# A hybrid convolution and gated-attention block: attention's output product as two sets of seven block products, with ScalarE in program order from the mixer's sets on

## The chip, the cores and the metric

The kernel runs on one core of one Trainium2 chip. The metric is the device time of one execution in microseconds (us), as the median of several runs. TensorE multiplies, VectorE (DVE) and ScalarE (ACT) work on tiles of 128 partitions, GpSimd (POOL) and SyncE (SP) mostly issue DMAs.

## The reference

One block works on 512 positions of width 1024, all in float32: a half-weighted SwiGLU, a mixer, a second SwiGLU and a last norm.

```python
x = x + 0.5 * swiglu(rmsnorm(x, g1), w_gu1, w_down1)        # 1024 -> 2 x 2816 -> 1024
h = rmsnorm(x, gm)
cb, cc, cu, q, k, v, g_lr, r, ga, gb = split(h @ w_in)
y_conv = (cb * causal_short_conv(cc * cu, conv_w)) @ w_out_conv
o = gla_chunked(q, k, v, log_sigmoid(g_lr @ gate_w_up + gate_b) / 16)   # 4 heads, chunks of 64
o = o * rsqrt(mean(o * o) + eps) * gla_norm_g                # per head, 256 wide
y_gla = (o * silu(r)) @ w_out_gla                            # 1024 x 1024
x = x + (sigmoid(ga) * y_conv + sigmoid(gb) * y_gla) @ w_o
x = x + 0.5 * swiglu(rmsnorm(x, g2), w_gu2, w_down2)
out = rmsnorm(x, gf)
```

## The kernel before, in words

**Layout.** Everything is held transposed: a tile has 128 features on its partitions and 512 positions along it. Each float32 operand is split into a rounded high part and the rest (`h`, `l`), and a product is three matmuls: high by high, high by low, low by high. ScalarE makes the high part (a CAST), VectorE the low part (a subtraction). For weights these are the tiles `wh` and `wl` (lines 328 and 329), three buffers each; for activations the tiles `op`, 14 buffers.

**Two kinds of product.** A *single* (`mm_single`, lines 351 to 359) makes 128 output features for all 512 positions: 8 blocks of the inner dimension by 3 matmuls, 24 matmuls of 512 columns, with one unit of split weights of 128 x 1024. A *set* (`Set` and `Operands`) makes 512 output features as a 2 by 2 block product by Winograd's form: seven block products named m1, p2, q6, p5, q7, p4, p3 instead of eight, each 24 matmuls of 256 columns (line 520) with a unit of split weights of its own. Some weights are sums of blocks: one sum is made by VectorE (line 313), three by DMAs that add in place, issued by POOL (line 303). Sums of activation blocks are made in place by VectorE (`Operands.sum`). Three of the products are copied out of PSUM by ScalarE (line 525); VectorE adds the quarters of the output (`quarter`, lines 1219 to 1230).

**The plan.** `PLAN` and `STEPS` list the weight units in the order of use. `Weights.take` issues the load, the split and the sums of a unit up to two steps ahead. SP issues all loads of weights. The order of one engine's instructions is otherwise made by a scheduler that works from modelled times; only in the last stage of the kernel is it written by hand (`tc.manual_schedule`).

**The mixer.** q, k and v come as singles and wide products. Then twelve sets follow (`MSETS`): the gates ga and gb, the convolution's inputs, cb and r. Attention's four heads are worked between the steps of these sets by hooks: `gates(h)`, `decays`, `scale(h)`, `scores(h)`, `state(h)`, `output(h)`, `squares(h)`. `gates` is a chain on ScalarE of Abs, Exp and Ln with a table load, and a scan on VectorE. The gates ga and gb are written to DRAM by DMAs that ScalarE issues. The last two sets are r: silu of r multiplies `O`, attention's output.

After the sets, w_out_conv is eight singles whose operands are the split of `Y` (line 1282: tiles `op` from tiles `y`). Each result is multiplied by sigmoid(ga), which SP loads into a temporary of the pool `tp` (six buffers). Meanwhile `O` is normalised by `r64`. Then w_out_gla is eight singles whose operands are the split of `O`; each result is multiplied by sigmoid(gb) and added into `m`. During the second of them x is reloaded from DRAM (`xs`) by POOL's DMAs. The split of `m` feeds w_o: one group of four outputs, then four singles. w_o's results are added to x.

Of the kernel before, what the change touches and what calls it, by code (L numbers as in the profile page):

```python
# [20 lines left out]
KF = DFF // P  # L21
HEADS = 4
# [168 lines left out]
def block_kernel(ctx: ExitStack, tc: tile.TileContext, xT, vecs, gf, gup, wgl, wts, out):  # L191
    nc = tc.nc
# [3 lines left out]
    front = ctx.enter_context(tc.tile_pool(name="front", bufs=1))  # L196
# [49 lines left out]
    x = [XS[0][:, k] for k in range(KD)]  # L246
# [237 lines left out]
    def newton_rsqrt(r, v, s, q):  # L484
        nc.scalar.activation(s, v, AF.Sqrt)
        nc.vector.reciprocal(s, s)
        nc.vector.tensor_tensor(out=q, in0=s, in1=s, op=ALU.mult)
        nc.vector.tensor_tensor(out=q, in0=q, in1=v, op=ALU.mult)
        nc.vector.tensor_scalar(out=q, in0=q, scalar1=-0.5, scalar2=1.5,
                                op0=ALU.mult, op1=ALU.add)  # L490
        nc.vector.tensor_tensor(out=r, in0=s, in1=q, op=ALU.mult)

    def mul(out_, a, b, eng=None):
        (eng or nc.vector).tensor_tensor(out=out_, in0=a, in1=b, op=ALU.mult)
# [359 lines left out]
    def mixer(norm, nxt):  # L854
        xh, xl = norm.h, norm.l
        cpool = pools["small"]
        xs = dram.tile([KD, P, S], F32, tag="xs", name="xs")
        gates_d = {n: dram.tile([KD, P, S], F32, tag=n, name=n) for n in ("ga", "gb")}
# [4 lines left out]
        Y = [tile_of("y", [P, 2, S + 2]) for _ in range(4)]  # L863
# [4 lines left out]
        def two(i):  # L868
            return flat(i).rearrange("p (e t) -> p e t", e=2)
# [6 lines left out]
        def G_tile(i, dtype=F32):  # L876
# [13 lines left out]
            out=maskf, in_=maskf, pattern=[[1, P]], compare_op=ALU.is_ge, fill=0.0,  # L890
# [21 lines left out]
        for i in range(6):  # L912
# [3 lines left out]
                                in1=gup_w[R2 : 2 * R2].bitcast(F32), op=ALU.subtract)  # L916
# [19 lines left out]
        def evac_k(h, o):  # L936
# [7 lines left out]
                                in1=glr[2 * R2 : R3].bitcast(F32), op=ALU.subtract)  # L944
# [27 lines left out]
        E, M, KS, EX, QS = (G_tile(i) for i in range(5))  # L972
# [6 lines left out]
        vs = cpool.tile([P, 16 * HEADS], F32, tag="vs", name="vs")  # L979
# [86 lines left out]
        O = [two(0), two(1), None, None]  # L1066
# [62 lines left out]
        OB = []  # L1129
# [45 lines left out]
        late = []  # L1175

        def finish_late():
            while late:
                late.pop(0)()
# [38 lines left out]
        def quarter(s, p):  # L1218

            bank, v = s.bank, s.v  # L1220
            if p not in ("p2", "q7", "p3"):
                return None
            t = T()
            if p == "q7":
                nc.vector.scalar_tensor_tensor(out=t, in0=bank["c"], scalar=-1.0, in1=v["q7"],
                                               op0=ALU.mult, op1=ALU.subtract)
            else:
                nc.vector.tensor_tensor(out=t, in0=bank["a" if p == "p2" else "c"],
                                        in1=v["m1" if p == "p2" else "q6"], op=ALU.add)
            return t  # L1230
# [42 lines left out]

            return Set(xo, done)

        run_sets(make, hooks=hooks)
        finish_late()


        def split_pair(v):  # L1280
            h, l = (tile_of("op", [P, 2, S], F32R) for _ in range(2))
            nc.scalar.copy(h, v)
            nc.vector.tensor_tensor(out=l, in0=v, in1=h.bitcast(F32), op=ALU.subtract)
            return [(h[:, i], l[:, i]) for i in range(2)]

        def parts(v):
            r = [hl for i in v for hl in split_pair(i)]
            return [a for a, _ in r], [b for _, b in r]

        def gate(name, d):  # L1290
            t = T()
            nc.sync.dma_start(t, gates_d[name][d])
            nc.scalar.activation(t, t, AF.Sigmoid)
            return t

        c_h, c_l = parts([Y[i][:, :, 2:] for i in range(4)])
        m = [two(d // 2)[:, d % 2] for d in range(KD)]

        n64 = [front.tile([P, HEADS * 16], F32, tag=t, name=f"{t}o") for t in
               ("st_v", "st_s", "st_r")]  # L1300
        r64, s64, q64 = n64
        newton_rsqrt(r64, vs, s64, q64)
        og = []
        for d in range(KD):
            t = gate("ga", d)
            yp = mm_single("w_out_conv", KD, d * P, c_h, c_l)
            mul(m[d], yp, t)
            if d % 2 == 0:
                h = d // 2
                tr, orow = E, M  # L1310
                nc.vector.tensor_copy(
                    tr.rearrange("p (b c) -> p b c", c=32),
                    r64[:, 16 * h : 16 * (h + 1)].unsqueeze(2).to_broadcast([P, 16, 32]))
                nc.vector.transpose(orow, tr)
                mul(O[h], O[h], orow.unsqueeze(1).to_broadcast([P, 2, S]))
        og_h, og_l = parts(O)
        m_h, m_l = [], []
        for d in range(KD):
            t = gate("gb", d)
            yp = mm_single("w_out_gla", KD, d * P, og_h, og_l)  # L1320
            if d == 1:
                XS.append(big("X2"))
                x[:] = [XS[-1][:, k] for k in range(KD)]
                for k in range(KD):
                    nc.gpsimd.dma_start(x[k], xs[k])
            mul(t, yp, t)
            nc.vector.tensor_tensor(out=m[d], in0=m[d], in1=t, op=ALU.add)
            if d % 2 == 1:
                for a, b in split_pair(two(d // 2)):
                    m_h.append(a)  # L1330
                    m_l.append(b)

        def evac(d, o):
            nc.vector.tensor_tensor(out=x[d], in0=o, in1=x[d], op=ALU.add)
# [72 lines left out]
```

## Time and profile before

| | |
|---|---|
| median of 3 runs | 1201.32 us (1201.03 to 1201.35) |
| profiled execution, whole | 1202.43 us |
| its span, first to last instruction | 1200.7 us |
| TensorE busy | 1191.5 us, 99% |
| VectorE busy | 799.2 us, 67% |
| ScalarE busy | 578.0 us, 48% |
| DMA | 184.48 MB, 154 GB/s on average |
| matmuls of 256 columns in sets (line 520) | 5040 |
| granted TensorE clock | 0.999 |

The profiled execution has a time of its own, 1202.43 us, of which the span is 1200.7. Views that are quoted later give a start in us from the beginning of the span, then a duration, the engine, the line, the operation, the output and input tiles, and in square brackets how long the engine sat idle before it and what ended that. A matmul's own duration overlaps with the next one's, so the pace of matmuls is read from the times between starts. Stages on the span: the mixer's sets end at 719.95 us, w_out_conv runs from there to 763.5, w_out_gla from 763.5 to 807.0, w_o and FFN2 follow.

### The profile page before, as it was taken

To read this page: it belongs to the slowest core of one execution; us is meant where nothing else is said; L and a number is where in the kernel's file an instruction comes from. 1 tells how busy PE (TensorE), PEld (TensorE's weight loads), DVE (VectorE), ACT (ScalarE), POOL (GpSimd) and SP (SyncE) were. 2 spreads that over 40 slices of the span, in tenths; PEclk is the share of its full clock that TensorE was granted. 3 is DMA by queue.
4 is the path that set the end of the run, shared out by engine and by line. 5 is a ranking of instruction groups with operands and counts; after the bars stand their busy time and mean duration, and the time that the engine had idled before them with its cause. 6 is when DMAs were issued, how large, how long until landed. Compare 5 with 4: busy or idle time off the path is not lost.

```text
span 1200.7 us, 18772 instructions
## 1 busy us (share of the span) xinstructions
PE 1191.5 (99%) x7714; PEld 1090.1 (91%) x7714; DVE 799.2 (67%) x960; ACT 578.0 (48%) x721; POOL 94.9 (8%) x131
## 2 busy tenths in 40 slices
PE   9999999999999999999999999999999999999997
PEld 7899999988888889999999998888889999998886
DVE  7976666832267864858678786455597666675685
ACT  6454454622153455646455464323346444562353
POOL 0011111000010000101101100100001111100100
PEclk9999999999999999999999999999999999999999
DMA  9377777532073316777777766614438777763431
GB/s 342 79 211 182 188 179 191 176 96 71 8 266 112 88 48 163 181 191 190 178 190 176 190 173 209 217 37 140 124 75 205 174 185 173 189 177 108 95 95 70
DMA packets 56741, 184.48 MB, mean 154 GB/s; under 512 B 6384, under 2 KB 10608, under 8 KB 56656
## 3 DMA queue, kind: packets, MB, share of 16 engines
q1 hardware_dynamic: 36912, 124.27, 30.3%
q0 software_dynamic: 15104, 54.53, 24.6%
q10 hardware_dynamic: 4640, 4.49, 1.2%
q8 instruction: 60, 0.98, 0.3%
q14 instruction: 25, 0.20, 0.0%
HBM read 124.55 MB, written 8.39 MB: 111 GB/s over the span
## 4 chain that ended last, share of the span: by engine, by line
PE 98%; ACT 1%; DMA 0%; DVE 0%; SPq 0%; issue 0%; ACTq 0%
PE mm L520 50%; PE mm L358 7%; PE mm L356 7%; PE mm L357 7%; PE mm L380 7%; PE mm L785 3%; PE mm L735 2%; PE mm L736 2%; PE mm L734 2%; PE mm L398 1%; PE mm L399 1%; PE mm L397 1%; PE aux L356 1%; PE aux L358 1%; PE aux L357 1%; PE aux L1076 1%
## 5 line engine op out<-in xcount | busy, mean ns | idle before, releaser
L520 PE MATMUL mm<-op,wh 128*128 128x256 f32 x3360 | 607.8, 284 | 0.3 <-ACT tp L525 0.3
L328 ACT CAST wh<-f 128x1024 fp32r<-128x1024 f32 (+1 forms) x313 | 327.1, 1046 | 490.2 <-PE mm L520 214.3
L329 DVE TENSOR_TENSOR wl<-f,wh 128x1024 fp32r<-128x1024 f32 (+1 forms) x313 | 380.4, 1218 | 251.7 <-ACT wh L328 238.1
L520 PEld LDWEIGHTS mm<-op,wh 128*128 128x128 f32 x3360 | 523.9, 192 | 1.3 <-ACT tp L525 0.5
L520 PE MATMUL mm<-op,wl 128*128 128x256 f32 x1680 | 475.6, 283 | 0.2 <-DVE wl L329 0.2
L520 PEld LDWEIGHTS mm<-op,wl 128*128 128x128 f32 x1680 | 321.8, 192 | 0.5 <-DVE wl L329 0.4
L356 PE MATMUL mm<-op,wh 128*128 128x512 f32 x388 | 151.3, 390 | 0.0
L358 PE MATMUL mm<-op,wl 128*128 128x512 f32 x388 | 151.2, 390 | 0.0
L357 PE MATMUL mm<-op,wh 128*128 128x512 f32 x388 | 151.0, 389 | 0.0
L303 POOL DMA_DIRECT2D f<-f x96 | 82.9, 864 | 845.4 <-DVE wl L329 460.1
L358 PEld LDWEIGHTS mm<-op,wl 128*128 128x128 f32 x388 | 72.8, 188 | 15.2
L357 PEld LDWEIGHTS mm<-op,wh 128*128 128x128 f32 x388 | 72.9, 188 | 15.2
L356 PEld LDWEIGHTS mm<-op,wh 128*128 128x128 f32 x388 | 72.8, 188 | 14.8
L380 PE MATMUL mm<-op,wh 128*128 128x512 f32 x256 | 63.8, 391 | 0.6 <-DVE op L431 0.4
L380 PEld LDWEIGHTS mm<-op,wh 128*128 128x128 f32 x256 | 47.7, 188 | 11.8 <-ACT wh L328 1.1
L525 ACT COPY tp<-mm 128x512 f32<-128x512 f32 x90 | 52.1, 579 | 0.0
L313 DVE TENSOR_TENSOR f<-f,f 128x1024 f32<-128x1024 f32 x32 | 39.1, 1223 | 0.8
L569 DVE TENSOR_TENSOR op<-hid,op 128x1024 fp32r<-128x1024 f32 x21 | 25.7, 1223 | 15.3 <-ACT op L568 15.3
L568 ACT CAST op<-hid 128x1024 fp32r<-128x1024 f32 x21 | 22.0, 1050 | 28.6 <-PE aux L735 20.7
L785 PE MATMUL mm<-wh,op 128*128 128x512 f32 x112 | 34.6, 389 | 0.0
L380 PE MATMUL mm<-op,wl 128*128 128x512 f32 x128 | 34.4, 391 | 0.0
L380 PEld LDWEIGHTS mm<-op,wl 128*128 128x128 f32 x128 | 23.9, 188 | 5.5 <-DVE wl L329 0.4
(252 smaller groups left out, 1152.2 us busy)
## 6 DMA issues: line engine op xcount, KB each, us to landing
f<-wts SPq DMA_DIRECT2D x219, 512.0 KB, 4.2
f<-f POOLq DMA_DIRECT2D x96, 512.0 KB, 5.0
X<-xT SPq DMA_DIRECT2D x8, 256.0 KB, 5.6
xs<-X POOLq DMA_DIRECT2D x8, 256.0 KB, 5.3
ga<-tp ACTq DMA_DIRECT2D x8, 256.0 KB, 4.3
gb<-tp ACTq DMA_DIRECT2D x8, 256.0 KB, 4.1
tp<-ga SPq DMA_DIRECT2D x8, 256.0 KB, 5.9
tp<-gb SPq DMA_DIRECT2D x8, 256.0 KB, 2.6
```

The source lines that it names most:

```text
L303: nc.gpsimd.dma_start(out_, a, accum_op=ALU.add)
L313: nc.vector.tensor_tensor(out=s3, in0=a11, in1=a21, op=ALU.add)
L328: nc.scalar.copy(h[:, :w], raw[:, :w])
L329: nc.vector.tensor_tensor(out=l[:, :w], in0=raw[:, :w], in1=h[:, :w].bitcast(F32), op=ALU.subtract)
L356: nc.tensor.matmul(o, wh, ah, start=first, stop=False)
L357: nc.tensor.matmul(o, wh, al, start=False, stop=False)
L358: nc.tensor.matmul(o, wl, ah, start=False, stop=last)
L380: nc.tensor.matmul(o[c], w[:, s : s + P], a[k], start=k == 0 and j == 0, stop=k == kt - 1 and j == 2)
L520: nc.tensor.matmul(to, ww[:, s], aa[:, t], start=fresh and k == 0 and e == 0 and j == 0, stop=k == 3 and j == 2, skip_group_check=True)
L525: nc.scalar.copy(v, o)
L569: nc.vector.tensor_tensor(out=lv, in0=v, in1=hv.bitcast(F32), op=ALU.subtract)
L785: nc.tensor.matmul(to, aa[:, c], ww, start=fresh and k == 0 and n == 0, stop=k == 3 and n == 2, skip_group_check=True)
```

## The change

w_out_gla becomes two sets of 512 outputs each. Their operands are blocks of `O`, which moves from four tiles to the flat view `Of`, and the sums are made in place in it; the operands m1, p2, p5 are made during w_out_conv. `O` is normalised head by head in the first four singles of w_out_conv, with two pairs of temporaries in turn. gb no longer goes through `tp`: quarters of it are loaded by SP into four fixed tiles (E, M, KS, EX), at steps that the table READ gives, and pass the sigmoid at steps that TAKE gives. The results are multiplied and added by quarters (`gla_add`), and `m` is split when a pair of its blocks is done. x is reloaded by SP after the first set's p3, not by POOL.

And from the mixer's twelve sets to the end of the new ones ScalarE runs in the order in which the code is written: the whole stretch stands under `tc.manual_schedule(engines={ENG.Activation})`. The other engines remain with the scheduler.

```diff
-    for d in range(KD):
-        units(single("w_out_gla", KD, d * P))
+    sets("w_out_gla", [(4 * i * P, (4 * i + 2) * P) for i in range(2)])
...
-        run_sets(make, hooks=hooks)
-        finish_late()
+        with tc.manual_schedule(engines={ENG.Activation}):
+            run_sets(make, hooks=hooks)
+            finish_late()
...
+            Of = OB[0].rearrange("p h e t -> p (h e) t")
+            oo = Operands(lambda j, l: Of[:, 4 * j : 4 * j + 4, half(l)])
+            AT = {3: "m1", 4: "p2", 6: "p5"}
             for d in range(KD):
                 t = gate("ga", d)
                 yp = mm_single("w_out_conv", KD, d * P, c_h, c_l)
                 mul(m[d], yp, t)
-            if d % 2 == 0:
-                h = d // 2
-                tr, orow = E, M
+                if d < HEADS:
+                    tr, orow = (E, M) if d % 2 else (KS, QS)
...
+                if d in AT:
+                    oo.make(AT[d])
+            oo.sum("q6")
-        og_h, og_l = parts(O)
-        for d in range(KD):
-            t = gate("gb", d)
-            yp = mm_single("w_out_gla", KD, d * P, og_h, og_l)
-            if d == 1:
...
-                    nc.gpsimd.dma_start(x[k], xs[k])
-            mul(t, yp, t)
-            nc.vector.tensor_tensor(out=m[d], in0=m[d], in1=t, op=ALU.add)
-            if d % 2 == 1:
-                for a, b in split_pair(two(d // 2)):
...
+            places = {(0, 0): E, (1, 1): M, (1, 0): KS, (0, 1): EX}
...
+            def gla_done(i):
+                def done(s, p):
+                    if not (i == 1 and p in ("q6", "p5", "q7")):
+                        finish_late()
+                    gla_add(i, s, p)
+                    if (i, p) in READ:
+                        fetch_gate(*READ[i, p])
+                    if (i, p) in TAKE:
+                        g = places[TAKE[i, p]]
+                        nc.scalar.activation(g, g, AF.Sigmoid)
+                return done
...
+            def reload():
...
+                    nc.sync.dma_start(x[k], xs[k])
+
+            run_sets(lambda i: Set(oo, gla_done(i)), hooks={(0, "p3"): [reload]})
+            finish_late()
```

Three places of the order that the prediction speaks of follow. Line numbers in the changed kernel are one lower there (327 for 328, 524 for 525, 1283 for 1282).

The first place is ScalarE's order at the end of the mixer's sets. `op<-y` are the high parts of w_out_conv's operands, `op<-O` of attention's output, `tp<-tp` and `tp<-mm` the silus of r, and wh_7073 (wh_7075 in the changed kernel) the first weights of w_out_conv. Before:

```order
L1282 CAST op_7147<-y_3387 128x1024
L1282 CAST op_7151<-y_3388 128x1024
L525 COPY tp_7027<-mm_6844 128x512
L328 CAST wh_7033<-f_6584 128x1024
L1243 ACTIVATE tp_7029<-tp_7029 128x512
L328 CAST wh_7073<-f_7065 128x1024
L1282 CAST op_7456<-O 128x1024
L328 CAST wh_7106<-f_7067 128x1024
L1243 ACTIVATE tp_7062<-tp_7062 128x512
L1237 ACTIVATE tp_7102<-mm_6844 128x512
L328 CAST wh_7170<-f_7069 128x1024
L1243 ACTIVATE tp_7135<-tp_7135 128x512
```

The same stretch of ScalarE in the changed kernel:

```order
L524 COPY tp_7029<-mm_6846 128x512
L1242 ACTIVATE tp_7031<-tp_7031 128x512
L327 CAST wh_7035<-f_6586 128x1024
L1242 ACTIVATE tp_7064<-tp_7064 128x512
L327 CAST wh_7075<-f_7067 128x1024
L1236 ACTIVATE tp_7104<-mm_6846 128x512
L327 CAST wh_7108<-f_7069 128x1024
L1242 ACTIVATE tp_7137<-tp_7137 128x512
L1283 CAST op_7141<-y_3385 128x1024
L1283 CAST op_7145<-y_3386 128x1024
L1283 CAST op_7149<-y_3387 128x1024
L1283 CAST op_7153<-y_3388 128x1024
```

All four casts of `op<-y` moved from ahead of the last copy of the sets (two of them stand still further up in the order before) to behind the last silu, tp_7137.

The second place is the hook `gates(2)` on ScalarE, after the second set's q6. tp_4541 (tp_4543) is q6's copy, wh_4552 (wh_4554) the first weights of the next set, the rows from `aux` to the third `g` the gate's Abs, Exp and Ln. Before:

```order
L328 CAST wh_4552<-f_4307 128x1024
L525 COPY tp_4541<-mm_4368 128x512
L987 ACTIVATE g_492_3614<-aux_4543,vec 128x512
L990 ACTIVATE g_492_3614<-g_492_3614 128x512
L991 ACT_TABLE_LOAD
L991 ACTIVATE g_492_3614<-g_492_3614 128x512
L328 CAST wh_4590<-f_4033 128x1024
L1004 ACT_TABLE_LOAD
```

ScalarE there in the changed kernel:

```order
L524 COPY tp_4543<-mm_4370 128x512
L986 ACTIVATE g_492_3614<-aux_4545,vec 128x512
L989 ACTIVATE g_492_3614<-g_492_3614 128x512
L990 ACT_TABLE_LOAD
L990 ACTIVATE g_492_3614<-g_492_3614 128x512
L327 CAST wh_4554<-f_4309 128x1024
L1249 DMA ga<-tp_4506 128x2x256
L327 CAST wh_4592<-f_4033 128x1024
```

And VectorE beside it in the changed kernel, where the third row is the scan and wl_4555 the low part of those weights:

```order
L987 TENSOR_SCALAR g_493_3615<-aux_4545,vec 128x512
L991 TENSOR_TENSOR g_493_3615<-g_493_3615,g_492_3614 128x512
L992 SCALAR_TENSOR_TENSOR g_492_3614<-reset,g_493_3615 128x512
L328 TENSOR_TENSOR wl_4555<-f_4309,wh_4554 128x1024
L997 TENSOR_TENSOR g_493_3615<-g_492_3614 128x512
```

The next set's first cast went from ahead of the copy to behind the gate's chain, and its low part now stands behind the scan.

The third place is TensorE's order where w_out_conv begins, in the changed kernel. The first row is the last matmul of the sets; mm_7169 is the first output of w_out_conv and mm_7215 the second, op_7141 and op_7142 are the high and low parts of the first operand.

```order
L519 MATMUL mm_6970<-op_4300,wl_7036 128x256
L355 MATMUL mm_7169<-op_7141,wh_7075 128x512
L355 MATMUL mm_7215<-op_7141,wh_7108 128x512
L356 MATMUL mm_7169<-op_7142,wh_7075 128x512
L357 MATMUL mm_7169<-op_7141,wl_7076 128x512
```

One matmul of the second output moved in ahead of the first that needs op_7142; otherwise w_out_conv's order is as before.

More of the change, by code (lines that the diff above doesn't have):

```diff
@@ L1274, in make @@
             return Set(xo, done)
-        run_sets(make, hooks=hooks)
-        finish_late()
[L1280 to L1303, printed above, removed]
@@ L1304, in mixer @@
-        for d in range(KD):
-            t = gate("ga", d)
-            yp = mm_single("w_out_conv", KD, d * P, c_h, c_l)
-            mul(m[d], yp, t)
-            if d % 2 == 0:
-                h = d // 2
-                tr, orow = E, M
[L1311 to L1315, printed above, removed]
@@ L1316, in mixer, with split_pair, parts, gate @@
-        og_h, og_l = parts(O)
-        m_h, m_l = [], []
-        for d in range(KD):
-            t = gate("gb", d)
-            yp = mm_single("w_out_gla", KD, d * P, og_h, og_l)
-            if d == 1:
+        with tc.manual_schedule(engines={ENG.Activation}):
+            run_sets(make, hooks=hooks)
+            finish_late()
+            def split_pair(v):
+                h, l = (tile_of("op", [P, 2, S], F32R) for _ in range(2))
+                nc.scalar.copy(h, v)
+                nc.vector.tensor_tensor(out=l, in0=v, in1=h.bitcast(F32), op=ALU.subtract)
+                return [(h[:, i], l[:, i]) for i in range(2)]
+            def parts(v):
+                r = [hl for i in v for hl in split_pair(i)]
+                return [a for a, _ in r], [b for _, b in r]
+            def gate(name, d):
+                t = T()
+                nc.sync.dma_start(t, gates_d[name][d])
+                nc.scalar.activation(t, t, AF.Sigmoid)
+                return t
+            c_h, c_l = parts([Y[i][:, :, 2:] for i in range(4)])
+            m = [two(d // 2)[:, d % 2] for d in range(KD)]
+            n64 = [front.tile([P, HEADS * 16], F32, tag=t, name=f"{t}o") for t in
+                   ("st_v", "st_s", "st_r")]
+            r64, s64, q64 = n64
+            newton_rsqrt(r64, vs, s64, q64)
+            Of = OB[0].rearrange("p h e t -> p (h e) t")
+            oo = Operands(lambda j, l: Of[:, 4 * j : 4 * j + 4, half(l)])
+            AT = {3: "m1", 4: "p2", 6: "p5"}
+            for d in range(KD):
+                t = gate("ga", d)
+                yp = mm_single("w_out_conv", KD, d * P, c_h, c_l)
+                mul(m[d], yp, t)
+                if d < HEADS:
+                    tr, orow = (E, M) if d % 2 else (KS, QS)
+                    nc.vector.tensor_copy(
+                        tr.rearrange("p (b c) -> p b c", c=32),
+                        r64[:, 16 * d : 16 * (d + 1)].unsqueeze(2).to_broadcast([P, 16, 32]))
+                    nc.vector.transpose(orow, tr)
+                    mul(O[d], O[d], orow.unsqueeze(1).to_broadcast([P, 2, S]))
+                if d in AT:
+                    oo.make(AT[d])
+            oo.sum("q6")
+            m_h, m_l = [None] * KD, [None] * KD
+            places = {(0, 0): E, (1, 1): M, (1, 0): KS, (0, 1): EX}
+            def fetch_gate(i, a, l):
+                d = 4 * i + 2 * a
+                nc.sync.dma_start(pair(places[a, l]), gates_d["gb"][d : d + 2, :, half(l)].rearrange(
+                    "e p t -> p e t"))
+            READ = {(0, "q6"): (1, 0, 0), (1, "m1"): (1, 1, 1), (0, "p3"): (1, 1, 0),
+                    (1, "q6"): (1, 0, 1)}
+            TAKE = {(0, "m1"): (0, 0), (0, "p5"): (1, 1), (0, "q7"): (1, 0), (0, "p4"): (0, 1),
+                    (1, "p5"): (1, 1), (1, "q7"): (0, 0), (1, "p2"): (1, 0), (1, "p4"): (0, 1)}
+            for a, l in places:
+                fetch_gate(0, a, l)
+            def gla_done(i):
[9 more added lines that the diff above has]
+                return done
+            def gla_add(i, s, p):
+                if p not in ("p2", "q7", "p4", "p3"):
+                    return
+                a, l = int(p in ("p4", "q7")), int(p in ("q7", "p3"))
+                d = 4 * i + 2 * a
+                g = places[a, l]
+                if p == "p4":
+                    nc.vector.scalar_tensor_tensor(out=g, in0=s.bank["b"], scalar=-1.0, in1=g,
+                                                   op0=ALU.mult, op1=ALU.mult)
+                else:
+                    mul(g, quarter(s, p), g)
+                y = two(d // 2)
+                nc.vector.tensor_tensor(out=y[:, :, half(l)], in0=y[:, :, half(l)], in1=pair(g),
+                                        op=ALU.add)
+                if p in ("p4", "p3"):
+                    def f():
+                        for j, (b, c) in enumerate(split_pair(y)):
+                            m_h[d + j], m_l[d + j] = b, c
+                    late.append(f)
+            def reload():
@@ L1324, in mixer @@
                 for k in range(KD):
-                    nc.gpsimd.dma_start(x[k], xs[k])
-            mul(t, yp, t)
-            nc.vector.tensor_tensor(out=m[d], in0=m[d], in1=t, op=ALU.add)
-            if d % 2 == 1:
-                for a, b in split_pair(two(d // 2)):
-                    m_h.append(a)
-                    m_l.append(b)
+                    nc.sync.dma_start(x[k], xs[k])
+            run_sets(lambda i: Set(oo, gla_done(i)), hooks={(0, "p3"): [reload]})
+            finish_late()
         def evac(d, o):
```

## The prediction

> **What bounds the kernel now.** I read the page first, its busy times and the chain that ended last.
>
> ```profile
> PE 1191.5 (99%) x7714; PEld 1090.1 (91%) x7714; DVE 799.2 (67%) x960; ACT 578.0 (48%) x721; POOL 94.9 (8%) x131
> PE 98%; ACT 1%; DMA 0%; DVE 0%; SPq 0%; issue 0%; ACTq 0%
> ```
>
> TensorE is busy 99% of the span and 98% of the chain. A busy matmul row says little about how fast matmuls follow each other, so the next view is who TensorE waited for in the whole span.
>
> ```profile
> PE aux L235 <- POOL ones L232: 1.1, 1, 1.1
> PE mm L380 <- DVE op L431: 0.4, 1, 0.4
> PE mm L520 <- ACT tp L525: 0.3, 1, 0.3
> PE mm L520 <- DVE wl L329: 0.2, 1, 0.2
> PE mm L380 <- ACT wh L328: 0.2, 1, 0.2
> ```
>
> That is 2.2 us in all. So the time changes in two ways only: the matmuls' own pace changes, or a wait appears that is not there now. Nothing can be won by removing waits. The pace comes from the chain in order of time and from VectorE's timeline, which shows when each product of the old stage was finished.
>
> ```profile
> 699.91 20.04 PE mm L520 x167
> 719.95 0.23 PE mm L356
> 941.49 20.16 PE mm L520 x168
> ```
>
> ```profile
> 741.77 0.69 DVE L494 TENSOR_TENSOR y<-mm,tp 128x512 f32<-128x512 f32 x1 [3.13 <-PE mm L358]
> 763.53 0.69 DVE L494 TENSOR_TENSOR y<-mm,tp 128x512 f32<-128x512 f32 x1 [2.00 <-PE mm L358]
> 807.05 0.69 DVE L494 TENSOR_TENSOR tp<-mm,tp 128x512 f32<-128x512 f32 x1 [2.89 <-PE mm L358]
> L494 DVE TENSOR_TENSOR tp<-mm,tp 128x512 f32<-128x512 f32 x8 | 5.5, 692 | 17.4 <-PE mm L358 17.4
> ```
>
> The last line groups the old stage's eight evacuations (763.5 to 807.1): every one waited for its matmuls. The mixer's sets end at 719.95 and the next matmul (L356) follows with no gap: call that moment T.
>
> **The matmuls.** Between 763.53 (the last product of w_out_conv) and 807.05 (the eighth of w_out_gla) lie eight products: 43.52 us, or 5.44 each, or 0.227 per matmul of 512 columns. A whole set in FFN2 is 168 matmuls of 256 columns in 20.16 us, 0.120 each. Two sets are 336 matmuls, 40.32 us. Saved: 43.52 - 40.32 = **3.2 us**. One block product in eight is saved, but two halves cost 0.240 where a whole costs 0.227. Bounds: the mixer's 167 in 20.04 us is the same pace, so 3.1 to 3.3.
> The Trainium skill (TensorE: Matmul & The Clock Gate, "Wait — 56ns, not 53.3ns?") has warm matmuls follow each other after N / 2.4 GHz plus about 2.5 ns. By that estimate 336 times 0.109 against 192 times 0.216 would save 4.7 us, 1.5 more, and the sum below would end at 1200.8; the trace's 0.120 stands against it.
>
> **The hand-over to w_out_conv.** These rows are ScalarE's and VectorE's around T.
>
> ```profile
> 706.94 1.05 ACT L1282 CAST op<-y 128x1024 fp32r<-128x1024 f32 x1
> 711.23 1.05 ACT L1282 CAST op<-y 128x1024 fp32r<-128x1024 f32 x1 [0.84 <-PE mm L520]
> 720.54 0.68 DVE L1228 TENSOR_TENSOR tp<-mm,tp 128x512 f32<-128x512 f32 x1
> 721.25 0.63 ACT L1243 ACTIVATE tp<-tp 128x512 f32<-128x512 f32 x1 [0.29 <-DVE tp L1228]
> 721.79 1.04 ACT L1282 CAST op<-O 128x1024 fp32r<-128x1024 f32 x1
> 741.55 1.06 ACT L328 CAST wh<-f 128x1024 fp32r<-128x1024 f32 x1 [1.12 <-PE mm L357]
> 742.64 1.23 DVE L329 TENSOR_TENSOR wl<-f,wh 128x1024 fp32r<-128x1024 f32 x1 [0.17 <-ACT wh L328]
> ```
>
> Before, the four casts of w_out_conv's operands (op<-y) are made while the last set runs; the last starts 8.7 us before T. In the new order all four stand behind the last silu of the sets, and that silu needs the last block product. So after T a chain runs that TensorE waits for: VectorE starts on the last quarter about 0.05 after T (741.77 against T plus four products, 741.72); the silu starts 0.71 later (720.54 to 721.25); the first cast 0.54 later (721.25 to 721.79); its low part 1.09 after that (741.55 to 742.64); this takes 1.23, and 0.05 to wake TensorE: 3.67 us. TensorE has two matmuls that need only the high part (0.45). Exposed: **3.2 us**. The other three casts and subtractions follow every 1.1 to 1.2 us where TensorE takes six matmuls, 1.36, for each, so they add nothing. Bounds: at least the four durations, 0.68 + 0.63 + 1.05 + 1.23 - 0.45 = 3.1; at most 4.4, if a weight's subtraction of 1.23 is in VectorE's way at T. I take 3.2: saving and wait cancel.
>
> **Program order at the mixer's gates.** A set's step is 24 matmuls, 2.88 us. The split weights have three buffers, so the cast for three steps on becomes possible when a step ends. Before, it went first. Now it is queued behind that step's copy and whatever the step's hook gives ScalarE. The longest of these is gates(2):
>
> ```profile
> 489.93 1.05 ACT L328 CAST wh<-f 128x1024 fp32r<-128x1024 f32 x1 [1.83 <-PE mm L520]
> 490.89 0.58 ACT L525 COPY tp<-mm 128x512 f32<-128x512 f32 x1
> 494.03 0.63 ACT L991 ACTIVATE g<-g 128x512 f32<-128x512 f32 x1
> 494.57 1.03 ACT L328 CAST wh<-f 128x1024 fp32r<-128x1024 f32 x1
> 494.69 0.69 DVE L992 TENSOR_TENSOR g<-g,g 128x512 f32<-128x512 f32 x1 [1.79 <-ACT g L991]
> 495.42 1.22 DVE L993 TENSOR_TENSOR_SCAN g<-reset,g 128x512 f32<-128x512 f32 x1
> 496.56 1.20 DVE L329 TENSOR_TENSOR wl<-f,wh 128x1024 fp32r<-128x1024 f32 x1
> ```
>
> The step ended at 489.9. If the copy starts there instead of at 490.89, everything comes 0.95 sooner, and the set's first cast takes the place of the row at 494.57: 493.6 to 494.7. Its subtraction stands behind the scan: 495.6 to 496.8. The gate's matmul takes 0.23 of TensorE, two steps 5.76, and the third matmul of the new set needs the low part at 489.9 + 0.23 + 5.76 + 0.24 = 496.1. Wait: **0.7 us**. The step has 5.76 + 0.24 - 1.05 - 1.23 = 3.7 us for ScalarE's other work; gates(3) takes the same 3.7, but its subtraction stands ahead of the scan there: 0. After gates(2), decays(2) and scale leave the next set's second weight about 0.1 late. Outputs, scores and squares hold ScalarE until TensorE's own aux matmuls are done, which moves the deadline too: 0. Bounds: 0 (the scheduler's order of VectorE holds some slack I don't see) to 1.9 (0.7 and a whole subtraction more).
>
> **Inside the new sets.** Casts rise from 8 to 14 weights and from 4 to 7 operands; copies, block sums and three SWDGE sums a set come on top. In the set's 20.16 us VectorE has 7 subtractions of weights and 2 to 5 of operands and 11 pieces of 512 columns. Such a piece starts 0.08 before the last one's end (495.42 + 1.22 against 496.56), so 1.14 and 0.61 each: 17 to 20 us, nearly full.
>
> ```profile
> 660.00:720.00 60.00, 60.00 (x501) 59.98 (x500) 46.86 (x52) 34.94 (x43) 5.17 (x6) 1.00 0.68 181
> 713.60 1.05 ACT L328 CAST wh<-f 128x1024 fp32r<-128x1024 f32 x1 [0.84 <-DMA f<-f]
> f<-f POOLq DMA_DIRECT2D x96, 512.0 KB, 5.0
> X<-xs POOLq DMA_DIRECT2D x8, 256.0 KB, 5.3
> 725.58 1.28 ACT L1293 ACT_TABLE_LOAD   x1 [2.75 <-DMA tp<-ga]
> ```
>
> The first line is the window of the mixer's last sets (the columns are PE, PEld, DVE, ACT, POOL busy): VectorE busy 78% there and TensorE without a wait, so the cover holds at this load; going through the new order by these durations, the tightest weight (p4 of the first set) still has about 2 us by my estimate. w_out_conv's third weight is cast behind the square root's and the sigmoid's two table loads: by T + 9.7 and subtracted by T + 11.4, wanted at T + 14.6. The gates (gb) come by SP into four fixed tiles, and so does the reload of x, which leaves POOL's queue and stands on SP ahead of three of those gates and four weights of w_o; they are wanted 8 us and more after the block sums let them start. The last sum of weights (a12 + a11) takes 5.0 us plus the issue; it is ready some 0.7 us ahead of the last step. At the end w_o's first two pairs of blocks are done, the last pairs have 10.9 us. I put 0.2 here for the bank that p4 leaves late; bounds 0 to 2.
>
> **Sum.** -3.2 + 3.2 + 0.7 + 0.1 + 0.2 = +1.0. The profiled execution took 1202.43 us for a span of 1200.7 and would take 1203.4 for 1201.7; its time is 1.1 above the median of the runs, 1201.32, so the median goes to **1202.3**. What a measurement here can tell from no change is about 0.2%, 2.4 us: 1198.9 to 1203.7. Own range of this case: 1201.0 to 1203.6.
>
> **The rivals.**
> *Program order costs at many hooks* (slower). Place: the mixer's twelve sets. Where ScalarE is held over 3.7 us after a step's end, the weight comes late; gates(2) lies on the edge. If four hooks (two gates, two decays) lose 0.7 each instead of one: +2.8 + 0.3 = 1204.4, up to 1206. For it: VectorE's order is made for modelled times. Against: at all other hooks I find 0 to 0.1. Chance 0.22.
> *The hand-over stays hidden* (faster). If TensorE finds c's parts ready at T, -3.2 + 1.0 or less: 1198.1 to 1199.1. Against: ScalarE's new order shows the casts behind the silu. 0.05.
> *Late transfers at the end of the new sets.* The reload (8 of 256 KB) and w_o's weights slow the last f<-f sum from 5.0 to 7 or 8 us, against 0.7 of slack: +1 to +2, 1203.3 to 1204.3. For it: the row at 713.60 already waits for such a sum. 0.07, half of it over the bound.
> *TensorE's clock falls in the gap.*
>
> ```profile
> 1193.32 0.39 PE L736 MATMUL aux<-op,op 128*128 128x512 f32 x1
> 1198.50:1199.00 0.50, 0.00 (x0) 0.00 (x0) 0.00 (x0) 0.00 (x0) 0.00 (x0) 1.00 0.98 389
> 1199.00:1199.50 0.50, 0.00 (x0) 0.00 (x0) 0.00 (x0) 0.00 (x0) 0.00 (x0) 0.52 0.24 90
> ```
>
> The column before the DMA share is the granted clock: it held for 5.3 us after the last matmul (1193.7 to 1199.0), then halved. The gap here is 2.4 us, two matmuls, and 0.8. If it did halve for one product, +5.4: 1207.7. 0.04.
> The Trainium skill (TensorE: Matmul & The Clock Gate, Part 1) puts the fall at one wholly idle free-running window of about 3.4 us; the trace's 5.3 agrees (between one and two windows), and an estimate from its 3.4 us to recover is +1.7.
>
> **How the numbers follow.** Forecast 0.62, within the bound; rivals 0.22, 0.05, 0.07, 0.04. Slower: 0.22 + 0.04 + 0.04 = 0.30. Faster: 0.04 of the 0.05. Same: the rest, 0.66. The range takes the forecast's lower end and most of the first and third rival: 1201.0 to 1205.2; left out are the hidden hand-over, the clock, and the rival's top.
>
> **What would show it.** Right: a wait of L355/L356 for the casts of op<-y of about 3.2 us in all just after the sets; L519 waiting 0.7 for a weight's low part (wl) right after gates(2); the new stage 40.3 us long. Wrong: TensorE without a gap at the hand-over; several waits of L519 for wh or wl in the mixer; the clock column under 1.00 after the hand-over; a wait in the last step of the new sets.

## The result and the profile after

The changed kernel takes **1203.59 us** in the median of 16 runs (1202.11 to 1204.97), the kernel before 1201.19 beside it (1200.22 to 1201.51). The ratio is **1.0021, 95% interval 1.0013 to 1.0028**: about 2.4 us slower. The profiled execution of the changed kernel took 1203.49 us for a span of 1201.8, with a mean granted clock of 0.997 (before 0.999). Of the ten executions of the first run of experiment 1 below, two took 2168 and 2853 us, its profiled one among them, so its ratio rests on the other eight and its profile is of a later run.

The page, busy times and the chain that ended last:

```profile
PE 1190.0 (99%) x7858; PEld 1096.5 (91%) x7858; DVE 819.4 (68%) x981; ACT 590.4 (49%) x736; POOL 95.9 (8%) x129
PE 97%; DVE 1%; ACT 1%; DMA 0%; issue 0%; POOL 0%; ACTq 0%; DVEq 0%; POOLq 0%
```

TensorE's share of the chain went from 98 to 97%, and VectorE and ScalarE now stand in it with 1% each. The whole list of TensorE's waits says where (total, times, longest):

```profile
PE mm L355 <- ACT op L1283: 2.5, 1, 2.5
PE aux L234 <- POOL ones L231: 1.1, 1, 1.1
PE mm L519 <- DVE wl L328: 0.7, 1, 0.7
PE mm L356 <- DVE op L1284: 0.5, 1, 0.5
```

The second one is in the kernel before too. The first and the fourth are the hand-over to w_out_conv. The third is gates(2), on TensorE's timeline:

```profile
495.36 0.39 PE L519 MATMUL mm<-op,wl 128*128 128x256 f32 x1 [0.75 <-DVE wl L328]
```

The chain in order of time (start, duration, what) shows the hand-over step by step and then the new sets:

```profile
719.44 0.61 DVE tp L1227
720.14 0.63 ACT tp L1242
720.77 0.94 ACT op L1283
721.73 1.24 DVE op L1284
...
767.90 40.31 PE mm L519 x336
808.21 21.79 PE mm L379 x96
```

The new sets run 40.31 us without a break, and w_o follows at once. TensorE's timeline around the hand-over (start, duration of the row, idle time before it in brackets):

```profile
719.02 0.28 PE L519 MATMUL mm<-op,wl 128*128 128x256 f32 x1
721.75 0.73 PE L355 MATMUL mm<-op,wh 128*128 128x512 f32 x2 [2.45 <-ACT op L1283]
723.01 0.80 PE L356 MATMUL mm<-op,wh 128*128 128x512 f32 x1 [0.53 <-DVE op L1284]
723.61 0.63 PE L357 MATMUL mm<-op,wl 128*128 128x512 f32 x1
724.04 0.63 PE L355 MATMUL mm<-op,wh 128*128 128x512 f32 x1
...
726.17 0.45 PE L357 MATMUL mm<-op,wl 128*128 128x512 f32 x1
726.46 0.39 PE L355 MATMUL mm<-op,wh 128*128 128x512 f32 x1
726.68 0.39 PE L356 MATMUL mm<-op,wh 128*128 128x512 f32 x1
```

From 723.6 to 726.2 a matmul starts every 0.43 us (723.61 to 724.04), afterwards every 0.22 to 0.23. The windows of TensorE there give the reason (stretch, its length, busy time and count, granted clock, DMA share, GB/s):

```profile
722.50:722.75 0.25, 0.00 (x0) 1.00 0.85 287
722.75:723.00 0.25, 0.00 (x0) 0.72 0.81 303
723.00:723.25 0.25, 0.23 (x1) 0.50 0.99 328
...
726.00:726.25 0.25, 0.25 (x2) 0.50 1.05 401
726.25:726.50 0.25, 0.25 (x3) 0.95 1.13 434
```

The clock halved at about 722.86 (0.72 is 0.44 of a quarter microsecond at full and the rest at half) and came back at about 726.27: 3.4 us. From 723.01 to 726.46 eight matmuls started where full pace takes 1.95 (below): about 1.5 lost.

**The account.** TensorE's first 75 us differ between executions, though the code and TensorE's order are the same there in every kernel: its 401st matmul starts at 74.18 in the profiled execution of before and at 72.59 in that of the changed kernel. (The list of before has waits of 0.4, 0.3, 0.2 and 0.2 in its first 60 us that are missing above.) So the sound measures are two stretches: from the start of that matmul to the sets' end on TensorE (the start of the last set's last matmul plus 0.12, its pace; the 719.95 given for before is the end of that matmul's row), and from there to the span's end.

| kernel | sets' end | span | 401st matmul to sets' end | sets' end to span's end | waits of TensorE in the last stretch |
|---|---|---|---|---|---|
| before | 719.79 | 1200.7 | 645.6 | 480.9 | none |
| changed | 719.14 | 1201.8 | 646.6 | 482.7 | 2.45 + 0.53, and the clock |
| early split | 719.66 | 1197.3 | 646.7 | 477.6 | none |
| gate moved too | 718.90 | 1196.5 | 646.6 | 477.6 | none |
| decays moved too | 719.00 | 1196.6 | 645.9 | 477.6 | none |
| order later | 719.52 | 1197.1 | 645.6 | 477.6 | none |
| 16 extra matmuls | 720.39 | 1201.5 | 646.6 | 481.1 | 0.53 + 0.53 beside them |
| 6 extra matmuls | 720.35 | 1201.5 | 646.5 | 481.2 | 1.73 + 0.53 |
| order alone | 719.88 | 1205.8 | 646.5 | 485.9 | 2.44 + 0.53, and the clock |

The kernels named in it are the experiments below. The sets save 480.9 - 477.6 = 3.3 (485.9 - 482.7 = 3.2 where both kernels have the hand-over's waits and the clock's fall). The hand-over costs 481.1 - 477.6 = 3.5. The clock costs 482.7 - 481.1 = 1.6. Together +1.8, and gates(2), in the first stretch, 1.0: +2.8, against 2.4 measured in the medians. The 0.4 between them is not accounted for.

### The profile page after: what moved, and what is told of

Same layout as the page of the kernel before. It is cut to its first block, busy times and chain, and to the rows that moved or that the text cites. A ratio compares the mean times of both kernels' runs of the same rounds, so it can differ in the third digit from the quotient of the medians.

```text
span 1201.8 us, 19117 instructions
## 1 busy us (share of the span) xinstructions
PE 1190.0 (99%) x7858; PEld 1096.5 (91%) x7858; DVE 819.4 (68%) x981; ACT 590.4 (49%) x736; POOL 95.9 (8%) x129
## 4 chain that ended last, share of the span: by engine, by line
PE 97%; DVE 1%; ACT 1%; DMA 0%; issue 0%; POOL 0%; ACTq 0%; DVEq 0%; POOLq 0%
PE mm L519 52%; PE mm L379 7%; PE mm L356 6%; PE mm L357 6%; PE mm L355 6%; PE mm L784 3%; PE mm L735 2%; PE mm L733 2%; PE mm L734 2%; PE mm L396 1%; PE mm L397 1%; PE mm L398 1%; PE aux L357 1%; PE aux L355 1%; PE aux L356 1%; PE aux L1075 1%
## 5 line engine op out<-in xcount | busy, mean ns | idle before, releaser
L519 PE MATMUL mm<-op,wh 128*128 128x256 f32 x3584 | 648.2, 283 | 0.0
L328 DVE TENSOR_TENSOR wl<-f,wh 128x1024 fp32r<-128x1024 f32 (+1 forms) x319 | 387.9, 1218 | 254.3 <-ACT wh L327 243.2
L519 PEld LDWEIGHTS mm<-op,wh 128*128 128x128 f32 x3584 | 559.3, 192 | 0.9
L327 ACT CAST wh<-f 128x1024 fp32r<-128x1024 f32 (+1 forms) x319 | 333.5, 1046 | 426.1 <-PE mm L519 152.7
L519 PE MATMUL mm<-op,wl 128*128 128x256 f32 x1792 | 507.6, 283 | 0.8 <-DVE wl L328 0.7
L519 PEld LDWEIGHTS mm<-op,wl 128*128 128x128 f32 x1792 | 343.5, 192 | 1.4 <-DVE wl L328 1.2
L302 POOL DMA_DIRECT2D f<-f x102 | 88.1, 864 | 896.8 <-DVE wl L328 530.3
L355 PE MATMUL mm<-op,wh 128*128 128x512 f32 x324 | 126.9, 392 | 2.5 <-ACT op L1283 2.5
L356 PE MATMUL mm<-op,wh 128*128 128x512 f32 x324 | 126.9, 392 | 0.5 <-DVE op L1284 0.5
L357 PE MATMUL mm<-op,wl 128*128 128x512 f32 x324 | 126.8, 391 | 0.0
L524 ACT COPY tp<-mm 128x512 f32<-128x512 f32 x96 | 56.0, 584 | 63.1 <-PE mm L519 63.1
L355 PEld LDWEIGHTS mm<-op,wh 128*128 128x128 f32 x324 | 61.1, 189 | 15.2 <-ACT op L1283 2.7
L356 PEld LDWEIGHTS mm<-op,wh 128*128 128x128 f32 x324 | 61.2, 189 | 13.7 <-DVE op L1284 1.0
L357 PEld LDWEIGHTS mm<-op,wl 128*128 128x128 f32 x324 | 61.3, 189 | 12.7
L379 PE MATMUL mm<-op,wh 128*128 128x512 f32 x256 | 63.7, 391 | 0.0
L379 PEld LDWEIGHTS mm<-op,wh 128*128 128x128 f32 x256 | 48.1, 189 | 10.2
L379 PE MATMUL mm<-op,wl 128*128 128x512 f32 x128 | 34.2, 389 | 0.0
L379 PEld LDWEIGHTS mm<-op,wl 128*128 128x128 f32 x128 | 24.0, 188 | 5.1
```

The costliest lines, as they stand in the source:

```text
L302: nc.gpsimd.dma_start(out_, a, accum_op=ALU.add)
L327: nc.scalar.copy(h[:, :w], raw[:, :w])
L328: nc.vector.tensor_tensor(out=l[:, :w], in0=raw[:, :w], in1=h[:, :w].bitcast(F32), op=ALU.subtract)
L355: nc.tensor.matmul(o, wh, ah, start=first, stop=False)
L356: nc.tensor.matmul(o, wh, al, start=False, stop=False)
L357: nc.tensor.matmul(o, wl, ah, start=False, stop=last)
```

## Experiments

**Theory A:** the hand-over, the clock's fall behind it and gates(2) ate the saving. **Rival B:** the loss lies in the new sets or their transfers. C to G are rivals in single places.

**1. Program order begins later.** The same code, but the `with` stands behind the split of w_out_conv's operands:

```diff
-        with tc.manual_schedule(engines={ENG.Activation}):
-            run_sets(make, hooks=hooks)
-            finish_late()
+        run_sets(make, hooks=hooks)
+        finish_late()
...
-            c_h, c_l = parts([Y[i][:, :, 2:] for i in range(4)])
+        c_h, c_l = parts([Y[i][:, :, 2:] for i in range(4)])
+        with tc.manual_schedule(engines={ENG.Activation}):
```

> Changed kernel, but ScalarE's program order begins only behind the split of w_out_conv's operands; the mixer's sets and the hand-over are left to the scheduler, as in the kernel before. Theory A (the hand-over wait of 3.0, the clock's fall of about 1.5 behind it and the gates' wait of 0.7 ate the saving of 3.2): all three go, 1201.2 - 3.2 + 0 to 0.4 = 1198.0 to 1198.4, TensorE without a wait over 0.5 but the first one, clock 0.999. Rival B (the loss is in the new sets' own work or in late transfers, the hand-over only shows it): still 1202 to 1203.6, with a wait in the new sets or a stretch of them longer than 40.3.

Measured: 1198.23 us, ratio 0.9975 (0.9965 to 0.9985). It was run again beside the last two experiments, for its profile:

> The kernel with program order only behind the split of w_out_conv's operands, beside the two others on one chip, for its profile: TensorE without a wait between the first 60 us and the end, w_out_conv 43.5 and the new sets 40.3 long; 1198.0 to 1198.4. Rival B: the new sets hold a wait of 0.3 or more, or are longer than 40.4.

Measured: 1197.88, ratio 0.9975 (0.9965 to 0.9985). TensorE's waits, all of them in the first 60 us:

```profile
PE aux L234 <- POOL ones L231: 1.1, 1, 1.1
PE mm L379 <- DVE op L430: 0.5, 1, 0.5
PE mm L379 <- ACT wh L327: 0.4, 2, 0.2
PE mm L519 <- DVE wl L328: 0.2, 1, 0.2
```

The new sets in its chain:

```profile
763.23 40.31 PE mm L519 x336
```

The median is 0.1 under the expected range. The new sets are as long as in the changed kernel, to the hundredth. Rival B falls: the sets' own work and transfers were covered in both.

**2. The splits alone.** Program order everywhere, but the four splits of w_out_conv's operands are written into the last set's steps, where `Y` is done:

```diff
+            for i, p in enumerate(("q6", "p5", "q7", "p2")):
+                hooks[(11, p)] = [lambda i=i: early_split(i)]
...
-            c_h, c_l = parts([Y[i][:, :, 2:] for i in range(4)])
+            c_h, c_l = [b for b, _ in cparts], [c for _, c in cparts]
```

> Changed kernel with program order over the whole stretch, but the four splits of w_out_conv's operands are written into the last mixer set's steps q6, p5, q7, p2, where Y is long done. Theory A: the waits of L355/L356 of 3.0 and the clock's fall of about 1.5 go, the gates' 0.7 stays: 1203.6 - 4.5 = 1199.1 (1198.7 to 1199.3), one wait of 0.7 on a weight's low part. Rival C (program order costs in many places, of which the hand-over is only the largest): 1200.5 or more, with new waits of the sets' matmuls on wh or wl, since four more casts and subtractions stand in the last set's steps.

Measured: 1198.94, ratio 0.9982 (0.9973 to 0.9991). TensorE's waits, beside the 1.1 for `ones` that every kernel here has:

```profile
PE mm L519 <- DVE wl L328: 1.0, 2, 0.8
```

And TensorE's timeline at the only one that is not in the first 60 us:

```profile
495.69 0.38 PE L519 MATMUL mm<-op,wl 128*128 128x256 f32 x1 [0.75 <-DVE wl L328]
```

The place of four casts in the order is worth 4.6 us, and the clock stays at 1.00 from 700 to 740. Rival C falls.

**3. The clock by itself.** Matmuls whose result is used nowhere fill part of the wait; the operands come no sooner:

```diff
+            busy = AUX()
+            for i in range(16):
+                nc.tensor.matmul(busy[:, :HW], ones_r, xo.parts["p3"][0][:, :HW],
+                                 start=True, stop=True)
             c_h, c_l = parts([Y[i][:, :, 2:] for i in range(4)])
```

> Changed kernel with 16 matmuls of 256 columns (0.12 each, 1.9 in all; their result is used nowhere) put on TensorE between the last set and w_out_conv, inside the wait of 2.5. Theory A (the clock falls because TensorE is idle most of 3.4 us): the clock stays at 1.00, the chain to the first cast and the arrival of L356's operand stay where they are, 1203.6 - 1.5 = 1202.1 (1201.7 to 1202.3). Rival D (no loss of clock to speak of; the 5 us that w_out_conv is longer are the wait and slower casts or weights): 1203.6 or more.

Measured: 1202.38, ratio 1.0012 (1.0003 to 1.0021), so 1.2 below the changed kernel and 0.1 above theory A's range. TensorE's timeline:

```profile
720.27 0.28 PE L519 MATMUL mm<-op,wl 128*128 128x256 f32 x1
720.39 2.08 PE L1299 MATMUL aux<-op,ones_r 128*128 128x256 f32 x16
723.00 0.73 PE L355 MATMUL mm<-op,wh 128*128 128x512 f32 x2 [0.53 <-ACT op L1283]
724.26 0.51 PE L356 MATMUL mm<-op,wh 128*128 128x512 f32 x1 [0.53 <-DVE op L1284]
724.60 0.39 PE L357 MATMUL mm<-op,wl 128*128 128x512 f32 x1
...
726.21 0.39 PE L355 MATMUL mm<-op,wh 128*128 128x512 f32 x1
```

Two of its windows, with the columns as above:

```profile
722.75:723.00 0.25, 0.00 (x1) 1.00 0.85 295
...
726.00:726.25 0.25, 0.25 (x3) 1.00 1.05 336
```

The first matmul that needs the first cast starts 2.73 after the last one of the sets, and the first low part is used at 3.99: both as in the changed kernel (719.02 to 721.75 and 723.01). The wait is the same, but the clock stays at 1.00, and the eight starts from 724.26 end at 726.21: 1.95 instead of 3.45. That is the clock's price, 1.5. Rival D falls. The fall was not the profiled execution's alone: eleven of the changed kernel's sixteen executions have a mean clock of 0.996 or 0.997, and with the 16 matmuls none of the eleven is under 0.998.

The same with 6 of these matmuls in place of 16:

> Changed kernel with 6 matmuls of 256 columns (0.7 us) in place of 16 on TensorE between the last set and w_out_conv: the idle stretch shrinks from 2.45 to 1.7 and the 0.53 stays. If the clock falls only when nearly all of about 3.4 us are idle, it stays at 1.00: 1202.2, as with 16. If being idle for most of the stretch is enough (now 2.2 idle in 4), it falls as before, 9 matmuls at 0.43: 1203.6. In both the waits' end stays 2.73 and 4.0 after the last set's last matmul.

Measured: 1203.45 (1201.58 to 1204.5), ratio 1.0019 (1.0010 to 1.0029). Its profiled execution took 1203.16 and kept the clock, with 1.73 us idle before L355 and the pace of 0.23 after it:

```profile
722.95 0.73 PE L355 MATMUL mm<-op,wh 128*128 128x512 f32 x2 [1.73 <-ACT op L1283]
...
724.54 0.39 PE L357 MATMUL mm<-op,wl 128*128 128x512 f32 x1
724.77 0.39 PE L355 MATMUL mm<-op,wh 128*128 128x512 f32 x1
```

Of its nine executions the four with a mean clock of 0.998 took 1201.58 to 1203.16, the five with 0.997 1203.45 to 1204.5. A fall in some executions and none in others would look like that, but the two groups adjoin and the page of only one execution is there; neither expectation is decided.

**4. The order alone.** The kernel before, w_out_gla still eight singles, with the same `with` around the stretch from the mixer's sets to w_out_gla's end.

> Kernel before (w_out_gla as eight singles) with ScalarE in program order from the mixer's sets to w_out_gla's end: the one part of the change without the other. Theory A: 1201.2 + 3.0 (hand-over) + 1.5 (clock) + 0.7 (gates) = 1206.4 (1205.9 to 1207.5, the upper end if attention's split waits in the same way at w_out_gla's start). Rival B (the order costs little by itself): 1202 or less.

Measured: 1207.50 (1205.53 to 1207.92), ratio 1.0048 (1.0036 to 1.0061): 6.4 above the kernel before on that chip (5.8 by the ratio), at the upper end of theory A's range. Its waits:

```profile
PE mm L356 <- ACT op L1283: 2.4, 1, 2.4
...
PE mm L520 <- DVE wl L329: 1.0, 2, 0.8
PE mm L357 <- DVE op L1284: 0.5, 1, 0.5
```

And the two windows of TensorE in which the clock fell and came back (the first is half a microsecond long):

```profile
724.00:724.50 0.50, 0.50 (x3) 0.62 0.59 201
...
727.50:727.75 0.25, 0.25 (x3) 0.92 0.81 311
```

The same three waits, without any set in w_out_gla; the one at w_out_gla's start, for which the upper end stood, did not come. By the stretches this kernel is 5.0 and 0.9 longer than before. The clock fell at about 724.12 and came back at about 727.54: again 3.4 us.

**5. The gates' wait.** To the early split is added that the next weights' cast is written ahead of gates(2), and then also ahead of decays(2) (`W.issue` issues the whole step of the weights, its load and sums with the cast):

```diff
-            (1, "q6"): [lambda: gates(2)], (1, "q7"): [decays], ...
+            (1, "q6"): [W.issue, lambda: gates(2)], (1, "q7"): [W.issue, decays], ...
```

The first one alone:

> The kernel with the early split, and in the hook after the second set's q6 the next weights' cast is written ahead of gates(2). Theory A (the wait of 0.75 after gates(2) is that cast standing behind the gate's chain and its subtraction behind the scan): the wait goes, 1198.9 - 0.75 = 1198.2 (1197.9 to 1198.5). Rival E (the subtraction stands behind the scan on VectorE anyway, or the gate's chain now ends late and its users wait): 1198.9 or more, with a wait of about 0.7 there or at the next hook.

Measured: 1198.61, ratio 0.9981 (0.9972 to 0.9990). That is 0.1 above theory A's range, and what rival E said of the next hook came: the wait is still there, later on TensorE's timeline:

```profile
500.78 0.38 PE L519 MATMUL mm<-op,wl 128*128 128x256 f32 x1 [0.74 <-DVE wl L328]
```

The chain just ahead of it:

```profile
498.84 0.75 DVE g L493 x2
499.59 1.15 DVE wl L328
```

And that weight's cast on ScalarE:

```profile
498.44 1.03 ACT L327 CAST wh<-f 128x1024 fp32r<-128x1024 f32 x1
```

The subtraction of this weight stands behind decays' products. Its cast, behind decays' chain on ScalarE, ended at 499.47, only 0.1 before those products, so both engines held it back alike. In the early split alone there was no wait here: TensorE came 0.75 later. Both:

> The kernel with the early split and the cast ahead of gates(2), and now also the cast that decays holds back is written ahead of it (hook after q7 of the same set), where the wait of 0.74 had moved to (500.8, a weight's low part behind decays' products on VectorE). Theory A' (each of these waits is one cast behind one hook's chain): no wait of TensorE between 480 and 510, 1198.6 - 0.75 = 1197.9 (1197.6 to 1198.2). Rival E' (VectorE's work of the two hooks, not ScalarE's order, makes some weight late): the wait moves on to the next step or set, 1198.6.

Measured: 1198.29, ratio 0.9976 (0.9966 to 0.9986). That is 0.1 above theory A's range. No wait between 60 us and the end is left, and the first stretch of the account falls from 646.6 to 645.9; that much of the theory is shown by the profile. The gain in the medians, 0.3, is under what these runs can tell.

**6. One early split of four.**

> As the kernel with the early split, but only the first of the four splits is made in the sets' steps; the other three stand behind the last silu. TensorE then has 11 matmuls (2.5 us) that need only the first pair. Theory A (the first split alone is what TensorE waits for; the rest follow in time): a wait of about 0.1 for the second pair's high part and 0.5 for its low part, no fall of the clock, 1198.9 + 0.6 = 1199.5 (1199.3 to 1199.9). Rival G (all four late splits cost, each by the 1.1 to 1.2 it takes): 1201 or more.

Measured: 1201.03, ratio 0.9998 (0.9990 to 1.0007): a miss by 1.5. TensorE's rows with a wait there:

```profile
717.27 0.39 PE L519 MATMUL mm<-op,wl 128*128 128x256 f32 x1 [0.57 <-DVE wl L328]
...
723.00 0.50 PE L355 MATMUL mm<-op,wh 128*128 128x512 f32 x1 [0.32 <-ACT op L1287]
723.35 0.40 PE L357 MATMUL mm<-op,wl 128*128 128x512 f32 x1
...
724.26 0.50 PE L356 MATMUL mm<-op,wh 128*128 128x512 f32 x1 [0.28 <-DVE op L1288]
```

The hand-over's waits are 0.6, as expected, but the stretch from the sets' end is 478.8, 1.2 above the early split's: a wait costs more than its idle time (last section). The 0.57 at 717.27 was in neither expectation: the last set's last sum of weights came late, and its cast with it, on ScalarE's timeline:

```profile
714.91 1.05 ACT L327 CAST wh<-f 128x1024 fp32r<-128x1024 f32 x1 [2.19 <-DMA f<-f]
```

In the changed kernel that cast started at 713.66 after 0.98 of waiting for the same sum. Whether the early cast or the DMAs of that execution made it later isn't settled. Rival G's 1201 was met, but not by its cause.

**7. No program order at all.**

> Changed kernel with no program order at all: the scheduler orders ScalarE in the mixer, in w_out_conv and in the new sets. Theory A (the sets save 3.2 wherever their casts come in time): the hand-over and gates(2) without a wait, 1198.2; but its order puts the sigmoids of gb, with table loads, ahead of several casts of w_out_conv's and the new sets' weights, so a wait of up to 1 to 2 on wh or wl there is possible: 1198.0 to 1200. Rival F (program order is needed in the new sets): waits in w_out_conv or the new sets of over 3, 1201 or more.

Measured: 1200.07, ratio 0.9992 (0.9984 to 1.0001), 2 us above experiment 1 in the same terms and 0.1 above theory A's range; rival F's 1201, with waits of over 3, was not met. TensorE's waits between 700 and 830, all in the new sets; between 60 and 700 there is none:

```profile
PE mm L519 <- ACT tp L524: 0.8, 2, 0.5
PE mm L519 <- DVE wl L328: 0.3, 1, 0.3
```

The larger part waits for copies out of PSUM (`tp`), which the expectation did not name. With what a wait costs beyond its idle time, about 0.25 in the sets, the three come to about 1.8 of the 2 us. So program order is of use in w_out_conv and the new sets, and costs in the mixer. The version with it only there (experiment 1) beats both kernels, at 0.9975 of before; the last one of experiment 5, at 0.9976, cannot be told from it.

## Why the prediction was right, and where it was not

*The matmuls, -3.2.* Right: -3.3 by the stretches, and the new sets took 40.31 us where 40.32 were forecast.

*The hand-over, +3.2.* Right in mechanism and nearly in size. From the end of the last set's matmul (719.02 + 0.28 = 719.30) to the first use of the low part (723.01) it took 3.71 against 3.67 forecast. By the stretches it cost 3.5; the list of waits shows only 3.0 of it. The 0.3 above the forecast is not in the chain: the prediction counted from the end of the last matmul's row, 0.16 after the next one would have started (0.28 against 0.12), and left out that the second start after a wait comes late (last section). Experiments 1 and 2 show the cause: with the casts ahead of the silu it is gone.

*gates(2), +0.7.* Right in place and cause: 0.75 of idle time, after this hook and no other; by the first stretch it cost 1.0. *decays and the bank, +0.3.* Neither showed: no wait after either. But the 0.1 for decays was too small taken alone: 0.74 when gates(2) no longer went before it (experiment 5).

*The clock.* This step failed. The prediction gave a fall 0.04, and a price of 5.4. It happened, in the profiled execution and in the order-alone kernel, and cost 1.5. Two things in that step were wrong. The chance rested on before's last microseconds, where the clock held for 5.3 us after the last matmul; that row is one sample of a time that varies, no bound: here the fall came 3.56 after the sets' last matmul (719.30 to 722.86), with two matmuls between. The price took a whole product at half pace, 24 matmuls; the clock came back after 3.4 us, and only eight starts were stretched. The Trainium skill (TensorE: Matmul & The Clock Gate, Part 1) gave the better size: the estimate from its 3.4 us to recover was +1.7. Its condition for the fall, an idle window of about 3.4 us, the trace does not bear out if idle means wholly idle, as the prediction has it: no idle stretch was longer than 2.45, and in the 3.4 us before the fall TensorE had run two matmuls, 0.73. In the order-alone kernel it had run for 1.1 us of the 3.4.

*The sum.* Forecast 1202.3, measured 1203.59: +0.2% of the time before, on the bound of 0.2% that was to separate no change from slower, with an interval (1.0013 to 1.0028) that reaches to both sides of it and leaves out 1. Against the forecast the clock is +1.5, the hand-over +0.3 and gates(2) +0.3; decays, the bank and the matmuls give 0.4 back. That is 1.7 where 1.3 was measured. The mechanism of the hand-over and of gates(2) was foreseen; that the time still lies inside the range is in part luck. The clock had been left out of the range with its price of 5.4, and the reach of the range above 1203.6 stood for program order at many hooks and for late transfers, neither of which came. A sign that the prediction gave for being wrong, the clock under 1.00 after the hand-over, did come. That the profiled execution of before lay above its median was allowed for, with about the right size: 1.1, against 1.2 over the sixteen executions.

*The other rivals.* Program order costs at many hooks: no, one wait. The hand-over stays hidden: no. Late transfers at the end of the new sets: no, w_o follows them without a gap (808.21).

## What to carry to other kernels

When an engine is put in the order of the code, look for casts that the scheduler had made early and that now stand behind a value finished last: the price is the whole chain from that value to the next stage's first operand. Write such casts where their inputs are done, and the order's gain elsewhere stays. A gap of TensorE is priced with its idle time, its restart and, as here after 2.45 us, two matmuls and a second gap, a stretch at half clock; how short a gap is safe these runs do not show. A wait that is removed may uncover the next one.

## What was not expected of the hardware

- The clock fell 0.38 us into a second gap, after one of 2.45 us and two matmuls (0.73), to 0.50 for 3.4 us (3.41 and 3.42 in the two kernels whose trace shows it). In the order-alone kernel it fell when TensorE was already at work again, with 1.1 us of matmuls in the 3.4 us before. With gaps of 0.53 and 0.53 it stayed; with 1.73 and 0.53 it stayed in the one execution that was profiled.
- A wait costs more than the idle time that the list gives, by about 0.28 between matmuls of 512 columns. Of that, 0.16 is the overlap: the list counts from the end of the last row, 0.39 after its start, where the next matmul would have started after 0.23. The other 0.12 is the second start after the wait, which at full clock comes 0.33 to 0.35 after the first (724.26 to 724.60 and 723.00 to 723.35 above), not 0.23. In experiment 6 two waits, 0.32 and 0.28, cost 1.2 so; at the hand-over 2.45 and 0.53 cost 3.5.
- In the profiled executions here, whose code and TensorE order are the same so far, the 401st matmul starts between 72.26 and 74.18 us, so spans of two profiles are better compared from a common point on.
